# Gate and up products of the feed-forward by one level of Strassen's identity, with the residual parked in DRAM

## The chip, the cores and the metric

The kernel runs on one core of a Trainium2 chip. The metric is the device time of one execution in microseconds (us), as the median of several executions. Five engines work side by side on the core: TensorE (PE in the profile, its weight loads PEld), VectorE (DVE), ScalarE (ACT), GpSimd (POOL) and SyncE (SP), which here only issues DMAs. They meet through semaphores alone.

## The reference

Two layers of a decoder trunk over 512 tokens of 1024 channels, in float32. Each layer has two feed-forward halves around a mixer of four attention branches:

```python
def swiglu(h, w_i, w_o):
    gate, up = jnp.split(h @ w_i, 2, axis=-1)     # h 512 x 1024, w_i 1024 x 5632
    return (jax.nn.silu(gate) * up) @ w_o         # w_o 2816 x 1024

for l in range(DEPTH):                            # DEPTH = 2
    x = x + 0.5 * swiglu(rms_norm(x, ffn1_norm[l]), ffn1_w_in[l], ffn1_w_out[l])
    ...                                           # one projection, four attentions, gates
    x = x + merged @ w_out[l]
    x = x + 0.5 * swiglu(rms_norm(x, ffn2_norm[l]), ffn2_w_in[l], ffn2_w_out[l])
```

The change concerns `h @ w_i`, which is computed four times (two per layer).

## The kernel before

**Layout.** Channels lie on the 128 partitions and tokens along the free axis, so the residual `x` is eight tiles of 128x512 (`NK` = 8), and they stay in SBUF. All products are made at float32 accuracy out of three passes of the `fp32r` type: each operand is split into a high part and a low remainder, and `mm3` (L231 to L236) adds high x high (L234), high x low (L235) and low x high (L236) into one PSUM tile. A weight tile of 128x512 holds four 128x128 blocks; `load_split` (L141) loads it by SP's queue (`raw`, 3 buffers), makes the high part on ACT (L147) and the low part on DVE (L150: raw minus high, both in SBUF). While `lo_parts["shared"]` is set, which is in the mixers only, every second low part is made on POOL.

**Feed-forward** (`ffn`, L253). The 2816 hidden channels are 22 blocks of 128 (`NH`). For each block `j`, called a unit here, `pg` gets 8 x 3 matmuls of 512 columns for the gate and `pu` as many for up. DVE multiplies both by `rb`, the reciprocal of the root mean square of each token (L265, L267), ACT takes the silu (L266), DVE multiplies gate and up (L268), and the result is split into `fh` (ACT, L271) and `fl` (DVE, L272). After the 22 units come eight output tiles `po` of 22 x 3 matmuls each, added to the residual (L278). The output phase already builds the operands of the stage after it: `Norm.add` squares each new residual tile into `ssq` (L181, L182) and splits it, scaled by the gain of the norm, into `xh` and `xl` (L188, L189). `Norm.finish` turns `ssq` into `rb` by one matmul with ones (L196), a square root on ACT (L198) and a reciprocal on DVE (L199).

**Order.** A scheduler places the instructions of each engine; the weight splits have a higher priority (`HP`), so that they run ahead as far as the four buffers of high and low parts allow. Each engine then takes its instructions strictly in that order.

The profile's names end in a letter for the half of a layer: `pga`, `pua`, `poa` belong to the first feed-forward of a layer, `pgb`, `pub`, `pob` to the second.

## Time and profile before

| | us |
|---|---|
| median of 3 executions (2688.86 to 2689.61) | 2688.99 |
| the profiled execution's own time | 2689.76 |
| its span, first to last instruction | 2688.0 |
| TensorE busy | 2669.4 |
| VectorE busy | 1486.0 |
| ScalarE busy | 1326.1 |
| GpSimd busy | 318.9 |

The four feed-forwards lie at about 8 to 375, 989 to 1349, 1349 to 1709 and 2324 to 2688 us of the span; between them are the two mixers with their output products. Busy time is the union of the instructions' own times. A matmul's own time is longer than its distance from the next one, because matmuls are pipelined; what a matmul costs in a full queue is the distance between two starts. `[… <-ACT xhf L188]` at the end of a row gives the idle time ahead of an instruction and what ended it.

### The profile page before, as it was taken

To read this page: it belongs to the slowest core of one execution; us is meant where nothing else is said; L and a number is where in the kernel's file an instruction comes from. 1 tells how busy PE (TensorE), PEld (TensorE's weight loads), DVE (VectorE), ACT (ScalarE), POOL (GpSimd) and SP (SyncE) were. 2 spreads that over 40 slices of the span, in tenths; PEclk is the share of its full clock that TensorE was granted. 3 is DMA by queue.
4 is the path that set the end of the run, shared out by engine and by line. 5 is a ranking of instruction groups with operands and counts; after the bars stand their busy time and mean duration, and the time that the engine had idled before them with its cause. 6 is when DMAs were issued, how large, how long until landed. Compare 5 with 4: busy or idle time off the path is not lost.

```text
span 2688.0 us, 36812 instructions
## 1 busy us (share of the span) xinstructions
PE 2669.4 (99%) x13054; PEld 2266.4 (84%) x13054; DVE 1486.0 (55%) x3028; ACT 1326.1 (49%) x2740; POOL 318.9 (12%) x438
## 2 busy tenths in 40 slices
PE   9999999999999999999999999999999999999999
PEld 7888889888888788888888888998888887888887
DVE  6444437777764564444354443487776646644432
ACT  4333347777665653333333333477776556433321
POOL 1000012222222200000000000222222222000000
PEclk9999999999999999999999999999999999999999
DMA  5333432222322332233322233322223223322233
GB/s 169 99 98 93 118 117 73 75 72 88 88 76 81 101 114 97 96 98 95 98 98 96 97 101 112 113 69 78 76 84 92 69 87 106 110 98 98 96 109 90
DMA packets 146488, 257.10 MB, mean 96 GB/s; under 512 B 17081, under 2 KB 47801, under 8 KB 146304
## 3 DMA queue, kind: packets, MB, share of 16 engines
q1 hardware_dynamic: 138960, 233.16, 28.1%
q0 software_dynamic: 6192, 19.50, 2.5%
q8 instruction: 102, 1.67, 0.3%
q10 hardware_dynamic: 1152, 2.10, 0.2%
q14 instruction: 82, 0.67, 0.1%
HBM read 248.31 MB, written 8.61 MB: 96 GB/s over the span
## 4 chain that ended last, share of the span: by engine, by line
PE 97%; DVE 1%; ACT 1%; issue 1%; DMA 0%; POOL 0%; ACTq 0%; POOLq 0%
PE pgl L234 4%; PE pgl L236 4%; PE pgl L235 4%; PE pga L235 3%; PE pua L234 3%; PE pua L236 3%; PE pua L235 3%; PE pga L236 3%; PE pga L234 3%; PE pob L236 3%; PE pub L234 3%; PE pgb L234 3%; PE pub L236 3%; PE poa L236 3%; PE pgb L236 3%; PE poa L235 3%
## 5 line engine op out<-in xcount | busy, mean ns | idle before, releaser
L234 PE MATMUL pgl<-xhm,higl 128*128 128x512 f32 x512 | 216.4, 423 | 0.0
L236 PE MATMUL pgl<-xhm,logl 128*128 128x512 f32 x512 | 200.9, 392 | 0.0
L235 PE MATMUL pgl<-xlm,higl 128*128 128x512 f32 x512 | 200.2, 391 | 0.0
L234 PE MATMUL pga<-xhf,higa 128*128 128x512 f32 x352 | 138.1, 392 | 3.0 <-ACT xhf L188 3.0
L150 DVE TENSOR_TENSOR loob<-rawob,hiob 128x512 fp32r<-128x512 f32 x96 | 62.0, 646 | 140.6 <-ACT hiob L147 140.6
L234 PE MATMUL pua<-xhf,hiua 128*128 128x512 f32 x352 | 137.9, 392 | 0.0
L235 PE MATMUL pga<-xlf,higa 128*128 128x512 f32 x352 | 137.4, 391 | 0.4 <-DVE xlf L189 0.4
L147 ACT ACTIVATE hiob<-rawob 128x512 fp32r<-128x512 f32 x96 | 57.3, 597 | 163.2 <-PE pob L235 138.3
L234 PE MATMUL pgb<-xhf,higb 128*128 128x512 f32 x352 | 137.8, 391 | 0.0
L235 PE MATMUL pua<-xlf,hiua 128*128 128x512 f32 x352 | 137.5, 391 | 0.0
L236 PE MATMUL pga<-xhf,loga 128*128 128x512 f32 x352 | 137.4, 390 | 0.0
L236 PE MATMUL pua<-xhf,loua 128*128 128x512 f32 x352 | 137.4, 390 | 0.0
L235 PE MATMUL pub<-xlf,hiub 128*128 128x512 f32 x352 | 137.0, 389 | 0.0
L234 PE MATMUL pub<-xhf,hiub 128*128 128x512 f32 x352 | 137.0, 389 | 0.0
L235 PE MATMUL pgb<-xlf,higb 128*128 128x512 f32 x352 | 137.0, 389 | 0.0
L236 PE MATMUL pub<-xhf,loub 128*128 128x512 f32 x352 | 137.0, 389 | 0.0
L235 PE MATMUL pob<-flb,hiob 128*128 128x512 f32 x352 | 136.9, 389 | 0.0
L234 PE MATMUL pob<-fhb,hiob 128*128 128x512 f32 x352 | 136.9, 389 | 0.0
L234 PE MATMUL poa<-fha,hioa 128*128 128x512 f32 x352 | 136.9, 389 | 0.0
L236 PE MATMUL poa<-fha,looa 128*128 128x512 f32 x352 | 136.9, 389 | 0.0
L236 PE MATMUL pgb<-xhf,logb 128*128 128x512 f32 x352 | 136.9, 389 | 0.0
L235 PE MATMUL poa<-fla,hioa 128*128 128x512 f32 x352 | 136.9, 389 | 0.0
(663 smaller groups left out, 7371.1 us busy)
## 6 DMA issues: line engine op xcount, KB each, us to landing
rawgl<-in_w_gate SPq DMA_DIRECT2D x128, 256.0 KB, 2.7
rawga<-in_f_in SPq DMA_DIRECT2D x88, 256.0 KB, 2.7
rawua<-in_f_in SPq DMA_DIRECT2D x88, 256.0 KB, 2.8
rawgb<-in_f_in SPq DMA_DIRECT2D x88, 256.0 KB, 2.7
rawub<-in_f_in SPq DMA_DIRECT2D x88, 256.0 KB, 2.8
rawoa<-in_f_out SPq DMA_DIRECT2D x80, 256.0 KB, 2.6
rawob<-in_f_out SPq DMA_DIRECT2D x80, 256.0 KB, 2.6
rawmo<-in_w_out SPq DMA_DIRECT2D x32, 256.0 KB, 2.8
```

The source lines that it names most:

```text
L147: A.activation(hi[:, :n], raw[:, :n], AF.Copy)
L150: eng.tensor_tensor(lo[:, :n], raw[:, :n], hi[:, :n].bitcast(F32), ALU.subtract)
L234: T.matmul(ps, wh, xh, start=first, stop=False)
L235: T.matmul(ps, wh, xl, start=False, stop=False)
L236: T.matmul(ps, wl, xh, start=False, stop=last)
```

## The change

Gate and up blocks of a unit are put one above the other, and so are the halves of the 1024 channels: the unit's weight is a 2 x 2 array of tiles of 128x512, `a11` and `a12` (gate, first and second half of the channels) and `a21`, `a22` (up). The operand is a 2 x 2 array as well: two halves of the channels (block `m` is paired with block `m + 4`) by two halves of the tokens (256 each). The eight block products are replaced by seven (`a`, `s`, `t`, `b`, `u`, `v`, `d`), each 4 x 3 matmuls of 256 columns:

- the sums of weights s1 to s4 are made on POOL, four additions of 128x512 per unit (L333); all seven weight tiles, four loaded and three or four summed, are then split as before on ACT (L311) and DVE (L312);
- the sums of the operand are made once per norm in `combine` (L224 to L236), which replaces the split for the two feed-forward norms: per pair of blocks, two scaled copies on ACT, four additions of 256 columns on DVE, and four high and low parts (three of 512 columns, one of 256);
- the seven results are added up in `after`: two are copied out of PSUM by ACT (L368, L374), five are read from PSUM by DVE in instructions of 256 columns (L371, L378, L381, L385, L389), two additions of 256 columns go to POOL (L382, L383). The products with `rb`, the silu and the split of the result are as before.

To make room for the seven-part operand, the residual leaves SBUF: it is written to DRAM after each stage and read back tile by tile in the next output phase, by POOL's queue. The merge of the mixer becomes a function of its own with its own buffers.

```diff
-        def split(self, m, xt):
-            g = pv[:, self.l, self.col + m:self.col + m + 1]
...
+            A.activation(r[0], x1, AF.Copy, scale=self.gain(p))
+            A.activation(r[1], x2, AF.Copy, scale=self.gain(p + HK))
+            V.tensor_tensor(r[2][:, lo], r[0][:, lo], r[0][:, hi], ALU.subtract)
+            V.tensor_tensor(r[2][:, hi], r[1][:, hi], r[2][:, lo], ALU.add)
+            V.tensor_tensor(r[3][:, lo], r[1][:, lo], r[2][:, hi], ALU.subtract)
+            V.tensor_tensor(r[0][:, hi], r[0][:, hi], r[1][:, hi], ALU.subtract)
...
+            for n in (0, 2, 1, 3):
+                w = S if n < 3 else TH
+                h = xh[:, n * S:n * S + w]
+                A.activation(h, r[n][:, :w], AF.Copy)
+                V.tensor_tensor(xl[:, n * S:n * S + w], r[n][:, :w], h.bitcast(F32), ALU.subtract)
...
+                    def plus(n, x, y):
+                        t = fp.tile([P, CW], F32, tag="ws", name=f"s{n}{nm}", bufs=4)
+                        with tc.high_priority(offset=HP):
+                            nc.gpsimd.tensor_tensor(t, x, y, ALU.add)
+                        return t
...
+                    s1 = plus(1, a21, a22)
+                    s2 = plus(2, s1, a11)
+                    s3 = plus(3, a11, a21)
+                    s4 = plus(4, s2, a12)
+                    self.w = dict(a=a11, s=s2, t=s1, b=a12, u=s3, v=s4, d=a22)
...
+                        make = (mm_tile, s_tile, mm_tile, t_tile)[made[0] % 4]
+                        self.ps[n] = make(f"p{n}{self.nm}")[:, :TH]
...
+                    for p in pairs:
+                        c = slice(p * P, (p + 1) * P)
+                        T.matmul(ps, wh[:, c], nrm.xh[p][:, sl], start=p == 0, stop=False)
+                        T.matmul(ps, wh[:, c], nrm.xl[p][:, sl], start=False, stop=False)
+                        T.matmul(ps, wl[:, c], nrm.xh[p][:, sl], start=False, stop=p == HK - 1)
...
+                    elif n == "u":
+                        self.dn = half("dn", nm)
+                        V.tensor_tensor(self.dn, ps, self.up, ALU.subtract)
+                        nc.gpsimd.tensor_tensor(self.up, self.up, self.p5, ALU.add)
+                        nc.gpsimd.tensor_tensor(self.u[:, TH:], self.dn, self.p5, ALU.subtract)
+                    elif n == "v":
+                        V.tensor_tensor(self.g[:, TH:], ps, self.up, ALU.add)
...
-                pg = mm_tile(f"pg{name}{j}")
-                chain(pg, w_in[l, j, 0], nrm.xh, nrm.xl, f"g{name}{j}")
-                pu = mm_tile(f"pu{name}{j}")
-                chain(pu, w_in[l, j, 1], nrm.xh, nrm.xl, f"u{name}{j}")
...
-                V.scalar_tensor_tensor(x[m], po, 0.5, x[m], ALU.mult, ALU.add)
...
+                nc.gpsimd.dma_start(xr, x_of[m])
...
+                V.scalar_tensor_tensor(xn, po, 0.5, xr, ALU.mult, ALU.add)
+                (nc.sync if nxt is None and m == NK - 1 else nc.gpsimd).dma_start(keep[m], xn)
```

VectorE within a unit, before, in the second feed-forward of a layer (`lo` are low parts of weights, `ub` and `gb` the results of up and gate, `flb` the low part of the product):

```order
L267 TENSOR_TENSOR ub_11765<-pub_11727,rbf_0_10339 128x512
L150 TENSOR_TENSOR loub_4_11833<-rawub_4_11830,hiub_4_11832 128x512
L268 TENSOR_TENSOR ub_11765<-ub_11765,gb_11764 128x512
L272 TENSOR_TENSOR flb_11771<-ub_11765,fhb_11770 128x512
L150 TENSOR_TENSOR logb_0_11862<-rawgb_0_11859,higb_0_11861 128x512
L265 TENSOR_TENSOR gb_11848<-pgb_11774,rbf_0_10339 128x512
L150 TENSOR_TENSOR logb_4_11880<-rawgb_4_11877,higb_4_11879 128x512
L150 TENSOR_TENSOR loub_0_11899<-rawub_0_11896,hiub_0_11898 128x512
```

Those eight are a whole unit. After the change, in the first feed-forward of a layer, a unit has sixteen; twelve of them in a row (`loaa` is the low part for product `a`, `pua` the result of product `u`, and so on; what ends in `_2849` or less belongs to the unit before):

```order
L312 TENSOR_TENSOR loaa_2950<-waa_2933,hiaa_2949 128x512
L381 TENSOR_TENSOR dna_2885<-pua_2872,upa_2827 128x256
L312 TENSOR_TENSOR losa_2969<-s2a_2943,hisa_2968 128x512
L385 TENSOR_TENSOR ga_2848<-pva_2893,upa_2827 128x256
L386 TENSOR_TENSOR ga_2848<-ga_2848,rbf_0_233 128x512
L312 TENSOR_TENSOR lota_2988<-s1a_2941,hita_2987 128x512
L389 TENSOR_TENSOR ua_2849<-pda_2913,dna_2885 128x256
L312 TENSOR_TENSOR loba_3009<-wba_2939,hiba_3008 128x512
L390 TENSOR_TENSOR ua_2849<-ua_2849,rbf_0_233 128x512
L312 TENSOR_TENSOR loua_3027<-s3a_2945,hiua_3026 128x512
L391 TENSOR_TENSOR ua_2849<-ua_2849,ga_2848 128x512
L371 TENSOR_TENSOR upa_2985<-p1a_2966,psa_2972 128x256
```

The instructions of 256 columns read one operand from PSUM and stand singly between those of 512 columns, which read both from SBUF.

GpSimd around the first feed-forward, before: between the DMAs of the set-up and those that follow the output phase there is nothing.

```order
L332 DMA scr_414<-flat 128x256
L332 DMA scr_416<-flat 128x256
L332 DMA scr_418<-flat 128x256
L332 DMA scr_420<-flat 128x256
L1124 DMA xs_3001<-x_104 128x512
```

GpSimd after, one unit and the start of the next:

```order
L333 TENSOR_TENSOR s1a_2941<-wca_2935,wda_2937 128x512
L333 TENSOR_TENSOR s2a_2943<-s1a_2941,waa_2933 128x512
L333 TENSOR_TENSOR s3a_2945<-waa_2933,wca_2935 128x512
L333 TENSOR_TENSOR s4a_2947<-s2a_2943,wba_2939 128x512
L382 TENSOR_TENSOR upa_2827<-upa_2827,p5a_2846 128x256
L383 TENSOR_TENSOR ua_2849<-dna_2885,p5a_2846 128x256
L333 TENSOR_TENSOR s1a_3099<-wca_3093,wda_3095 128x512
```

All six read both operands from SBUF; L385 on VectorE waits for L382, and L390 for L383.

VectorE where the second feed-forward of layer 0 ends and the first of layer 1 begins, before:

```order
L278 SCALAR_TENSOR_TENSOR xn_10326<-pob_12969,xn_10326 128x512
L150 TENSOR_TENSOR loua_4_13149<-rawua_4_13146,hiua_4_13148 128x512
L182 TENSOR_TENSOR ssqf_1_10342<-ssqf_1_10342,sqf_1_7_13073 128x512
L189 SCALAR_TENSOR_TENSOR xlf_1_7_13077<-xn_10326,pv,xhf_1_7_13076 128x512
L150 TENSOR_TENSOR loga_0_13178<-rawga_0_13175,higa_0_13177 128x512
L199 RECIPROCAL rbf_1_13083<-rbf_1_13083 128x512
```

and after:

```order
L418 SCALAR_TENSOR_TENSOR xnb_16557<-pob_16454,xrb_16452 128x512
L201 TENSOR_TENSOR ssqf_1_15616<-ssqf_1_15616,sqf_1_7_16560 128x512
L226 TENSOR_TENSOR rf_1_3_2_16565<-rf_1_3_0_16563 128x256
L227 TENSOR_TENSOR rf_1_3_2_16565<-rf_1_3_1_16564,rf_1_3_2_16565 128x256
L229 TENSOR_TENSOR rf_1_3_0_16563<-rf_1_3_0_16563,rf_1_3_1_16564 128x256
L228 TENSOR_TENSOR rf_1_3_3_16566<-rf_1_3_1_16564,rf_1_3_2_16565 128x256
L236 TENSOR_TENSOR xlf_1_3_16574<-rf_1_3_1_16564,xhf_1_3_16573 128x512
L236 TENSOR_TENSOR xlf_1_3_16574<-rf_1_3_2_16565,xhf_1_3_16573 128x512
L246 RECIPROCAL rbf_1_16586<-rbf_1_16586 128x512
L236 TENSOR_TENSOR xlf_1_3_16574<-rf_1_3_0_16563,xhf_1_3_16573 128x512
L236 TENSOR_TENSOR xlf_1_3_16574<-rf_1_3_3_16566,xhf_1_3_16573 128x256
L312 TENSOR_TENSOR loaa_16617<-waa_16600,hiaa_16616 128x512
```

The reciprocal, which before stood behind the low parts of the first unit, now stands ahead of the first of them (`loaa`). On TensorE the matmul with ones that feeds it stands directly behind the last matmul of the output phase and ahead of product `a`.

## Rows read from the trace of the kernel before

**Rows 1.** The page: span, engines' busy time, and the chain that ended last.

```profile
span 2688.0 us, 36812 instructions
...
PE 2669.4 (99%) x13054; PEld 2266.4 (84%) x13054; DVE 1486.0 (55%) x3028; ACT 1326.1 (49%) x2740; POOL 318.9 (12%) x438
...
PE 97%; DVE 1%; ACT 1%; issue 1%; DMA 0%; POOL 0%; ACTq 0%; POOLq 0%
```

**Rows 2.** Busy time by stretch: stretch, us, engines (instructions), granted clock, DMA share, GB/s.

```profile
1000.00:1220.00 220.00, 220.00 (x973) 182.21 (x971) 107.50 (x166) 77.89 (x123) 0.00 (x0) 1.00 0.30 99
...
8.40:14.00 5.60, 5.17 (x11) 3.76 (x12) 5.60 (x12) 5.49 (x10) 0.00 (x0) 0.50 0.95 333
```

**Rows 3.** Timeline of TensorE, up product, 512 columns: start us, us, instruction.

```profile
99.69 0.39 PE L235 MATMUL pua<-xlf,hiua 128*128 128x512 f32 x1
...
100.83 0.39 PE L234 MATMUL pua<-xhf,hiua 128*128 128x512 f32 x1
```

**Rows 4.** Timeline of TensorE in a mixer, matmuls of 256 columns.

```profile
779.28 0.28 PE L364 MATMUL pt0d<-hit0d,xlm 128*128 128x256 f32 x1
...
780.12 0.28 PE L362 MATMUL pt0d<-hit0d,xhm 128*128 128x256 f32 x1
```

**Rows 5.** Timeline of VectorE, one unit of a feed-forward.

```profile
1099.38 0.69 DVE L267 TENSOR_TENSOR ub<-pub,rbf 128x512 f32<-128x512 f32 x1 [1.54 <-PE pub L236]
1099.99 0.68 DVE L150 TENSOR_TENSOR loub<-rawub,hiub 128x512 fp32r<-128x512 f32 x1
...
1110.27 0.69 DVE L267 TENSOR_TENSOR ub<-pub,rbf 128x512 f32<-128x512 f32 x1 [1.54 <-PE pub L236]
```

**Rows 6.** Groups of ScalarE in 1000 to 1220 us: count, busy us, mean ns.

```profile
L147 ACT ACTIVATE hiub<-rawub 128x512 fp32r<-128x512 f32 x41 | 25.9, 632 | 67.4 <-PE pub L235 65.0 <-PE pub L236 2.4
```

**Rows 7.** GpSimd: group of 512 columns in the whole span, then one of 256.

```profile
L150 POOL TENSOR_TENSOR logl<-rawgl,higl 128x512 fp32r<-128x512 f32 x64 | 83.6, 1306 | 253.8 <-ACT higl L147 227.9 <-DVE acc L632 13.1 <-DMA rawgl<-in_w_gate 4.7
...
777.46 0.74 POOL L150 TENSOR_TENSOR lot0d<-rawt0d,hit0d 128x256 fp32r<-128x256 f32 x1 [0.87 <-ACT hit0d L147]
```

**Rows 8.** Timelines of VectorE and GpSimd where the two meet in a mixer.

```profile
718.62 1.29 DVE L634 TENSOR_TENSOR acc<-acc,gt 128x512 f32<-128x512 f32 x1
...
718.35 1.02 POOL L150 TENSOR_TENSOR lot0d<-rawt0d,hit0d 128x384 fp32r<-128x384 f32 x1 [4.73 <-ACT hit0d L147]
...
552.87 0.68 DVE L150 TENSOR_TENSOR logl<-rawgl,higl 128x512 fp32r<-128x512 f32 x1
...
553.40 1.30 POOL L150 TENSOR_TENSOR logl<-rawgl,higl 128x512 fp32r<-128x512 f32 x1 [4.67 <-ACT higl L147]
```

**Rows 9.** Single lines of VectorE: duration ns min/median/max, first and last start.

```profile
L632 DVE TENSOR_TENSOR gt<-pbr,gt x48: 670/690/693, 672.4 to 2284.5; 128x512 f32<-128x512 f32 x48
...
L634 DVE TENSOR_TENSOR acc<-acc,gt x48: 671/691/1499, 673.8 to 2285.2; 128x512 f32<-128x512 f32 x48
...
L576 DVE TENSOR_TENSOR o0B<-po0B,oc0B x12: 407/422/428, 541.0 to 661.4; 64x256 f32<-64x256 f32 x12
```

**Rows 10.** Timelines of TensorE and ScalarE at the start.

```profile
8.42 0.80 PE L234 MATMUL pga<-xhf,higa 128*128 128x512 f32 x1 [3.04 <-ACT xhf L188]
...
7.65 0.72 ACT L188 ACTIVATE xhf<-x,pv 128x512 fp32r<-128x512 f32 x1 [2.53 <-DMA pv<-in_pv]
```

**Rows 11.** Timelines between two feed-forwards: TensorE, VectorE, ScalarE.

```profile
1349.42 0.39 PE L234 MATMUL pga<-xhf,higa 128*128 128x512 f32 x1
...
1349.62 0.69 DVE L278 SCALAR_TENSOR_TENSOR xn<-pob,xn 128x512 f32<-128x512 f32 x1 [0.23 <-PE pob L236]
...
1351.01 0.70 DVE L182 TENSOR_TENSOR ssqf<-ssqf,sqf 128x512 f32<-128x512 f32 x1
...
1357.06 0.69 ACT L198 ACTIVATE rbf<-pnf,epsc 128x512 f32<-128x512 f32 x1 [2.96 <-PE pnf L196]
...
1357.78 3.35 DVE L199 RECIPROCAL rbf<-rbf 128x512 f32<-128x512 f32 x1 [4.26 <-ACT rbf L198]
```

More of the change, by code (lines that the diff above doesn't have):

```diff
@@ L168, in __init__, with open, close, order @@
             self.l, self.col, self.name = l, PV[which], name
+            self.pairs = which != "nm"
             self.xh, self.xl = [], []
-            self.ssq = per.tile([P, S], F32, tag="ssq", name=f"ssq{name}")
+            self.kept = {}
+        def open(self):
+            self.pool = tc.tile_pool(name=f"x{self.name}", bufs=1, side="right", reuse_waits="tile")
+            self.xp = self.pool.__enter__()
+            self.ssq = per.tile([P, S], F32, tag="ssq", name=f"ssq{self.name}")
+        def close(self):
+            self.pool.__exit__(None, None, None)
+        def order(self):
+            return [m // 2 + m % 2 * HK for m in range(NK)] if self.pairs else range(NK)
         def add(self, m, xt, alloc):
             self.square(m, xt, alloc)
-            self.split(m, xt)
+            self.split(m, xt, alloc)
         def square(self, m, xt, alloc):
@@ new lines, in ffn @@
+            for j in range(NH):
+                t = Hidden(j)
+                if j == 0:
+                    for n in "ast":
+                        t.product(n, range(HK - 1))
+                for n in "astbuvd":
+                    t.product(n, range(HK - 1, HK) if j == 0 and n in "ast" else range(HK))
+                    t.after(n)
+            nrm.close()
+            if nxt is not None:
+                nxt.open()
+            for n, m in enumerate(nxt.order() if nxt is not None else range(NK)):
+                if n == 1 and early is not None:
+                    early()
+                xr = fp.tile([P, S], F32, tag="g", name=f"xr{name}{m}")
+                nc.gpsimd.dma_start(xr, x_of[m])
@@ L1090, in mixer @@
                 ml.append(lo)
-            xn = []
-            for m in range(NK):
-                xr = sb_tile(f"xr{l}{m}")
+            for m in nxt.order():
+                xr = mp.tile([P, S], F32, tag="xr", name=f"xr{l}{m}", bufs=3)
                 nc.gpsimd.dma_start(xr, xs[m])
@@ L1121, in trunk_kernel @@
         nxt.finish_cols()
[L1122 to L1124 removed]
         nrm, nxt = nxt, Norm(l, "n2", f"f2_{l}")
[L1126 removed]
+        x = kept(f"xt{l}")
+        with tc.tile_pool(name=f"acc{l}", bufs=1, reuse_waits="tile") as ap:
+            acc = []
+            mixer(l, nrm, ap, acc)
+            nrm.close()
+            nxt.open()
+            merge(l, acc, nxt, xs, x)
```

167 lines of the change are left out of this document (115 added, 52 removed).

## The prediction

> **What bounds the kernel now.** The page comes first: TensorE is busy for 2669.4 of 2688.0 us and 97% of the chain that ended last is TensorE; VectorE is busy 55%, ScalarE 49%, GpSimd 12% [rows 1]. A change that takes columns from TensorE therefore pays, as long as nothing else becomes later. The second view is the busy time by stretch, because those shares are averages: in 220 us inside a gate-and-up phase VectorE has 107.50 us, ScalarE 77.89 and GpSimd nothing at all, at a granted clock of 1.00 [rows 2]. GpSimd works in the mixers only. The third view are the timelines of one unit. VectorE's L267 returns after 1110.27 − 1099.38 = 10.89 us [rows 5]; that is one unit, and there are 4 x 22 = 88 of them, 958 us in all. Five matmul starts lie 1.14 us apart, 0.228 us each [rows 3], and 48 of these are 10.94 us: a unit is TensorE's time.
>
> **The change, TensorE.** A unit gets 7 x 4 x 3 = 84 matmuls of 256 columns for 48 of 512. The mixers have such matmuls, each with a weight load of its own as here: seven starts in 0.84 us, 0.120 us each [rows 4]. So 84 x 0.120 = 10.08 us: 0.81 us less per unit, 71 us over 88 (2.6%), and not an eighth of 958, since half the columns cost more than half the time.
> The page "TensorE: Matmul & The Clock Gate" of the Trainium skill (section "Back-to-back issue gap") gives a gap of columns over 2.4 GHz plus 2.5 ns, which is 109 and 216 ns here; by it 84 would be 9.17 us and 48 would be 10.36, an estimate of 104 us saved. The rows show 120 and 228 ns, and they decide.
>
> **VectorE and ScalarE, per unit.** VectorE has eight instructions of 512 columns now. After: seven low parts of weights, and as before `rb` twice, gate times up, and `flb`: eleven of 512 columns, all reading both operands from SBUF, plus five of 256 columns that read one from PSUM. Two that wait for nothing start 1099.99 − 1099.38 = 0.61 us apart [rows 5]; 11 x 0.61 = 6.7 us. The 256-column kind takes 0.42 [rows 9], 0.34 with the same overlap of 0.08; 5 x 0.34 = 1.7. Together 8.4 us, below 10.08. ScalarE: nine of 512 columns at 0.63 [rows 6] and two copies of 256 columns, which cost no more than that each, so at most 11 x 0.63 = 6.9 us. Both would hide under TensorE if each engine stood alone.
>
> **GpSimd, per unit.** Four additions of 512 columns at 1.30 and two of 256 at 0.74 [rows 7, 8]: 6.7 us, which also is below 10.08. But GpSimd and VectorE don't stand alone, and this is the step on which the forecast rests. Where they meet in a mixer, L634 (both operands in SBUF) takes 1.29 instead of its median of 0.69: GpSimd's instruction ends at 718.35 + 1.02 = 719.37, VectorE's at 718.62 + 1.29 = 719.91, 0.54 us later [rows 8, 9]. The other way round, GpSimd starts at 553.40 while VectorE runs until 553.55 and ends at 554.70, 1.15 us after it [rows 8]. So the two exclude each other for 0.54 of VectorE's 0.69 us and for 1.15 of GpSimd's 1.30; only the first 0.15 us of either can lie beside the other. L632, with one operand in PSUM, shows nothing of it: 48 instructions, the longest 0.693, where L634's longest is 1.499 [rows 9]. I take 0.74 − 0.15 = 0.59 for GpSimd's 256 columns.
>
> **The sum for a unit.** Exclusive time: 11 x 0.54 + 4 x 1.15 + 2 x 0.59 = 5.94 + 4.60 + 1.18 = 11.72 us. That alone is above TensorE's 10.08 and above the 10.89 of before. It is the lower bound; it needs all five PSUM instructions and every wait to lie under GpSimd's work. The upper bound lets nothing lie beside anything: 8.41 + 5.78 = 14.19. In between decides VectorE's order. The PSUM instructions stand singly between the others, so a 1.15 us hold can hide one of them (0.34) and then stops the next low part. I let two of the four sums meet one: 4.60 − 0.68 = 3.92. The two small additions stand on a loop: L382 can only start when `dn` (L381) is made, VectorE's L385 waits for it one instruction later, and L383 follows at once and stops L386; I count 0.74 of wait and hold there and 0.15 for the rest, 0.9. So 8.41 + 3.92 + 0.9 = 13.2 us. VectorE then is late for TensorE's low parts, and the four buffers of high and low parts (4 x 12 x 0.120 = 5.8 us of matmuls) run empty within a few units. Per unit 13.2 − 10.89 = +2.31, over 88 units **+203 us**.
>
> **Starts and seams.** Before, the first matmul follows the first split at 8.42 [rows 10], at half the clock: 11 of them in 8.40 to 14.00 [rows 2], worth 2.5 us at full clock, so a full-speed start would be 11.5. After, VectorE's list ahead of the first low part of a weight has 39 instructions: 16 sums of 256 columns (5.4), the low parts of four pairs (12 x 0.61 + 4 x 0.34 = 8.7) and seven squares (4.3), 18.4 us from 7.65 on, and half of the first four sums on GpSimd, 2.3 us: first product at 28.4, **+17**. At the three seams into a paired norm the next product now waits for the whole norm, since on VectorE the reciprocal stands ahead of the first low part: residual 0.23 + 0.69, square 0.63, sum 0.70, root 0.69, reciprocal 3.35 [rows 6, 11], two low parts and the first weight's (0.61 + 0.34 + 0.61), and some 0.5 us (an estimate) for the matmul with ones: 7.8 us and hand-overs, where before the next product had begun 0.2 us before that residual [rows 11]. I take 8.2 each, **+25**. The first unit of each phase finds no weights prepared: 2 us each (an estimate from three low parts), **+8**. I let the residual's reads and writes cost nothing: they are issued in output phases, where an output tile takes 66 x 0.228 = 15 us and GpSimd has no arithmetic. Without that cover a read would cost at most a few us per phase. The mixers' code is the same, 0.
>
> **Sum:** 2688 + 203 + 17 + 25 + 8 = 2941 us of span. The profiled execution's own time was 1.8 above its span and 0.8 above the median of the runs, so a median lies some 1 us above the span: **2942 us**, 9% slower. A measurement of this kernel tells 0.2% (5 us) from no change.
>
> **Rivals.**
> *TensorE stays the bound (the other side).* The exclusion might cost VectorE less: below 10.08 − 8.41 = 1.67 us per unit of the 5.78 that GpSimd holds, VectorE keeps up, and from there TensorE decides: 2688 − 71 + 50 + 1 = 2668 us, faster by 0.8%. For it: all three engines' own sums are below 10.08, and no row of a feed-forward shows GpSimd at work. Against it: exclusive time alone needs 11.72, and L634 and the pair at 553 us fit it to a few hundredths. Chance 0.13.
> *The port at its floor.* If the scheduler's order happens to interleave, a unit is 11.7 to 12.5 us: 2688 + 73 + 30 + 1 = 2792 (with cheaper seams) to about 2880. For it: in the rows GpSimd takes its turn at the next boundary of VectorE's instructions, so neither starves. Against it: VectorE takes its instructions in order. Chance 0.10.
> *Whole instructions exclude each other*, the first 0.15 us too, and VectorE meets every one: 8.41 + 4 x 1.30 + 2 x 0.74 = 15.1 us per unit, 2688 + 370 + 50 + 1 = 3109 us. Rows 8 speak against it, the chain of L382 to L386 for something near it. Chance 0.09.
> The page "SBUF — State Buffer" (section "SBUF: two separate sides") states this as a rule: VectorE's instruction with two SBUF inputs and GpSimd's share a port pair as an exclusive lock for the whole instruction. By that rule the exclusive time of a unit would be 11 x 0.69 + 6.68 = 14.3 us; the rows let 0.15 us of each overlap, hence my 11.72.
> *The clock falls.* TensorE would wait for a quarter of each unit. After 3.04 us without work [rows 10] it was granted 0.50, the 1.2 GHz level [rows 2]. At that level 84 matmuls take some 20 us and the kernel about 3550. Against it: a product of 1.4 us stands between any two waits, and no wait of a unit comes near 3 us. Chance 0.02.
>
> **How the numbers follow.** The forecast (12.5 to 14.2 us per unit, 2880 to 3035) has 0.66. The range of 8 in 10 takes it in, with most of the floor's case and the lower edge of the whole-instruction case: 2790 to 3055. Faster by over 0.2% is the first rival, 0.13; slower are the others, 0.86; 0.01 is left for no change.
>
> **What would show it.** In the profile after: units of VectorE about 13 us apart; low parts (L312) and L386, L390 of up to 1.8 us beside GpSimd's L333, while L378 or L389 stay at 0.4; VectorE nearly without idle time, TensorE's gaps ended by DVE at L312; 256-column starts 0.120 apart within a product. I am wrong if VectorE shows idle time ended by TensorE, if L312's median stays at 0.69 with its longest below 1, or if TensorE's share stays near 99%.

## The result

The changed kernel takes 2956.48 us, median of 4 runs, against 2689.08: a ratio of 1.0992, 95% interval 1.0973 to 1.1011. The forecast was 2942, the range 2790 to 3055. The profiled execution took 2953.4 us with a span of 2951.6, that is 263.6 us over the span of before.

The page of the changed kernel: span, busy time, the chain that ended last, and one of the groups (out<-in, shapes, count, busy us, mean ns, idle time before).

```profile
span 2951.6 us, 46110 instructions
...
PE 2710.2 (92%) x16222; PEld 2392.5 (81%) x16222; DVE 2156.0 (73%) x3828; ACT 1524.5 (52%) x3245; POOL 1052.4 (36%) x1022
...
PE 60%; DVE 24%; issue 12%; POOL 3%; ACT 1%; DMA 0%; DVEq 0%; POOLq 0%; ACTq 0%
...
L333 POOL TENSOR_TENSOR s3b<-wab,wcb 128x512 f32<-128x512 f32 x44 | 73.5, 1670 | 72.7 <-DVE loub L312 72.7
```

Against [rows 1], TensorE's share of the chain fell from 97% to 60%, and VectorE and "issue" (time in which the profile shows no wait) hold most of what it lost. GpSimd's instructions of 512 columns, 1.30 us in [rows 7], now take 1.67 us in the mean of this group. The shares are averages again; the stretch inside one gate-and-up phase says it better. Windows of the changed kernel (as in [rows 2]: stretch, us, TensorE, weight loads, VectorE, ScalarE, GpSimd with instructions, granted clock, DMA share, GB/s):

```profile
1100.00:1320.00 220.00, 184.96 (x1401) 171.01 (x1400) 208.72 (x268) 95.39 (x186) 133.79 (x102) 1.00 0.26 81
1017.50:1022.00 4.50, 4.15 (x9) 2.86 (x10) 4.47 (x9) 3.63 (x7) 0.00 (x0) 0.50 0.12 43
1075.20:1085.00 9.80, 5.93 (x24) 5.32 (x25) 6.28 (x8) 2.46 (x5) 1.28 (x1) 0.50 0.16 54
```

In the first line VectorE is at 208.72 of 220 us, where it had 107.50, TensorE at 184.96, and the clock stays at 1.00. The other two lines are the starts of a merge and of a phase, at half the clock; they come up below.

One unit of VectorE, from one low part of product `t` to the next, and GpSimd beside it (start us, us, engine, line, tiles; in brackets the idle time before it and what ended it). A hold is the time by which an instruction takes longer than it does alone:

```profile
1198.91 1.78 DVE L312 TENSOR_TENSOR lotb<-s1b,hitb 128x512 fp32r<-128x512 f32 x1
1200.61 0.41 DVE L389 TENSOR_TENSOR ub<-pdb,dnb 128x256 f32<-128x256 f32 x1
1200.94 1.71 DVE L312 TENSOR_TENSOR lobb<-wbb,hibb 128x512 fp32r<-128x512 f32 x1
1202.58 0.68 DVE L390 TENSOR_TENSOR ub<-ub,rbf 128x512 f32<-128x512 f32 x1
...
1204.39 0.41 DVE L371 TENSOR_TENSOR upb<-p1b,psb 128x256 f32<-128x256 f32 x1
1204.72 1.45 DVE L312 TENSOR_TENSOR lovb<-s4b,hivb 128x512 fp32r<-128x512 f32 x1
...
1206.70 1.78 DVE L312 TENSOR_TENSOR lodb<-wdb,hidb 128x512 fp32r<-128x512 f32 x1
...
1210.97 0.42 DVE L385 TENSOR_TENSOR gb<-pvb,upb 128x256 f32<-128x256 f32 x1 [0.63 <-POOL upb L382]
1211.43 0.75 DVE L386 TENSOR_TENSOR gb<-gb,rbf 128x512 f32<-128x512 f32 x1
1212.10 1.78 DVE L312 TENSOR_TENSOR lotb<-s1b,hitb 128x512 fp32r<-128x512 f32 x1
```

```profile
1198.40 1.74 POOL L333 TENSOR_TENSOR s1b<-wcb,wdb 128x512 f32<-128x512 f32 x1
1200.82 1.29 POOL L333 TENSOR_TENSOR s2b<-s1b,wab 128x512 f32<-128x512 f32 x1 [0.68 <-POOL s1b L333]
1203.94 1.68 POOL L333 TENSOR_TENSOR s3b<-wab,wcb 128x512 f32<-128x512 f32 x1 [1.83 <-DVE loub L312]
1206.31 1.62 POOL L333 TENSOR_TENSOR s4b<-s2b,wbb 128x512 f32<-128x512 f32 x1 [0.68 <-POOL s3b L333]
```

The unit returns after 1212.10 − 1198.91 = 13.19 us. Four low parts are held, by 1.10, 1.03, 0.77 and 1.10 us over their 0.68, together 4.00. Each ends 0.55 us after the addition that held it: `s1b` ends at 1198.40 + 1.74 = 1200.14, `lotb` at 1200.69. L371, which reads one operand from PSUM, lies wholly under `s3b` and takes its 0.41 us. The one wait of the unit is that of L385 for the small addition on GpSimd, 0.63 us.

Who waited for VectorE in 1080 to 1360 us, one phase (waiter, waited for, us in total, times, longest):

```profile
PE ptb L362 <- DVE lotb L312: 15.7, 19, 0.8
```

Where the 263.6 us lie, by the first TensorE start of each stage before and after (a seam is the place between two stages at which TensorE waits for a norm):

| stage | before | after | more | forecast |
|---|---|---|---|---|
| to the first product | 8.42 | 29.73 | 21.3 | |
| four gate-and-up phases | 967.6 | 1158.4 | 190.9 | |
| setup matmuls, moved from the first phase to its output phase | | | 3.3 | |
| these three together | | | 215.5 | 17 + 203 + 8 = 228 |
| three gaps at the seams | 0 | 10.3 + 7.4 + 10.3 | 28.0 | 25 |
| two mixers and the rest of their merges | 1229.3 | 1249.4 | 20.1 | 0 |

### The profile page after: what moved, and what is told of

Read it like the earlier page. It is cut to its first block, busy times and chain, and to the rows that moved or that the text cites. A ratio compares the mean times of both kernels' runs of the same rounds, so it can differ in the third digit from the quotient of the medians.

```text
span 2951.6 us, 46110 instructions
## 1 busy us (share of the span) xinstructions
PE 2710.2 (92%) x16222; PEld 2392.5 (81%) x16222; DVE 2156.0 (73%) x3828; ACT 1524.5 (52%) x3245; POOL 1052.4 (36%) x1022
## 4 chain that ended last, share of the span: by engine, by line
PE 60%; DVE 24%; issue 12%; POOL 3%; ACT 1%; DMA 0%; DVEq 0%; POOLq 0%; ACTq 0%
PE pgl L281 4%; PE pgl L282 4%; PE pgl L283 4%; PE poa L281 3%; PE poa L283 3%; PE pob L283 3%; PE poa L282 3%; PE pob L282 3%; PE pob L281 3%; DVE lotb L312 2%; DVE lota L312 2%; DVE loda L312 2%; DVE lodb L312 2%; POOL upb L382 1%; POOL upa L382 1%
## 5 line engine op out<-in xcount | busy, mean ns | idle before, releaser
L153 POOL TENSOR_TENSOR logl<-rawgl,higl 128x512 fp32r<-128x512 f32 x64 | 83.0, 1297 | 260.4 <-ACT higl L150 225.9
L153 DVE TENSOR_TENSOR looa<-rawoa,hioa 128x512 fp32r<-128x512 f32 x96 | 62.0, 645 | 122.6 <-ACT hioa L150 120.7
L283 PE MATMUL pob<-fhb,loob 128*128 128x512 f32 x352 | 137.1, 390 | 0.0
L150 ACT ACTIVATE hiob<-rawob 128x512 fp32r<-128x512 f32 x96 | 57.0, 596 | 150.6 <-PE pob L282 132.5
L150 ACT ACTIVATE hioa<-rawoa 128x512 fp32r<-128x512 f32 x96 | 57.0, 596 | 146.1 <-PE poa L282 112.5
L283 PEld LDWEIGHTS pgl<-xhm,logl 128*128 128x128 f32 x512 | 96.4, 188 | 23.1
L281 PEld LDWEIGHTS pgl<-xhm,higl 128*128 128x128 f32 x512 | 97.6, 191 | 17.1
L150 ACT ACTIVATE higl<-rawgl 128x512 fp32r<-128x512 f32 x128 | 80.6, 630 | 58.8 <-PE pgl L282 38.8
L282 PEld LDWEIGHTS pgl<-xlm,higl 128*128 128x128 f32 x512 | 97.3, 190 | 14.2
L394 ACT ACTIVATE fha<-ua 128x512 fp32r<-128x512 f32 x44 | 27.8, 633 | 144.9 <-DVE ua L391 144.9
L394 ACT ACTIVATE fhb<-ub 128x512 fp32r<-128x512 f32 x44 | 27.8, 633 | 144.4 <-DVE ub L391 87.0
L333 POOL TENSOR_TENSOR s3b<-wab,wcb 128x512 f32<-128x512 f32 x44 | 73.5, 1670 | 72.7 <-DVE loub L312 72.7
L333 POOL TENSOR_TENSOR s3a<-waa,wca 128x512 f32<-128x512 f32 x44 | 73.1, 1662 | 73.3 <-DVE loua L312 73.3
```

Source lines behind the costliest of these rows:

```text
L150: A.activation(hi[:, :n], raw[:, :n], AF.Copy)
L153: eng.tensor_tensor(lo[:, :n], raw[:, :n], hi[:, :n].bitcast(F32), ALU.subtract)
L281: T.matmul(ps, wh, xh, start=first, stop=False)
L282: T.matmul(ps, wh, xl, start=False, stop=False)
L283: T.matmul(ps, wl, xh, start=False, stop=last)
L333: nc.gpsimd.tensor_tensor(t, x, y, ALU.add)
```

## The experiments

A unit is the time from one instruction of VectorE to the same one of the next unit, or, where TensorE has no gap, a phase divided by 22.

| run | us | ratio to before (95%) | a unit, us |
|---|---|---|---|
| sums on VectorE | 2772.59 | 1.0308 (1.0292 to 1.0323) | 11.12 |
| no sums | 2693.85 | 1.0015 (1.0006 to 1.0025) | 10.08 |
| copies on GpSimd | 2728.61 | 1.0146 (1.0130 to 1.0163) | 10.46 |
| before, with additions | 2699.06 | 1.0033 (1.0020 to 1.0045) | 10.9 |
| parking alone | 2738.13 | 1.0178 (1.0163 to 1.0194) | 11.24 |
| the same, 32 bytes on | 2716.05 | 1.0098 (1.0083 to 1.0113) | 11.03 |
| the same, 96 bytes on | 2704.02 | 1.0053 (1.0038 to 1.0069) | 10.92 |
| no sums, 32 bytes on | 2678.49 | 0.9956 (0.9942 to 0.9971) | 9.90 |
| sums in PSUM, 32 bytes on | 2684.51 | 0.9977 (0.9968 to 0.9986) | 9.89 |
| the same, late norm, 96 bytes on | 2690.28 | 1.0005 (0.9997 to 1.0014) | 10.08 |
| the same, late norm, 32 bytes on | 2677.73 | 0.9952 (0.9939 to 0.9966) | 9.90 |
| the same, TensorE kept busy | 2680.45 | 0.9964 (0.9952 to 0.9977) | 9.9 |

The first four runs ask whether the shared port is the cause, the next three what parking the residual costs by itself, the others whether the products can win.

### The four sums on VectorE

```diff
-                            nc.gpsimd.tensor_tensor(t, x, y, ALU.add)
+                            V.tensor_tensor(t, x, y, ALU.add)
```

> The changed kernel with one word altered: the four sums of 512 columns per unit (L333) are issued on VectorE instead of GpSimd. Theory (shared port): an addition costs VectorE 0.61 us of its own time, where on GpSimd it cost the pair about 1.0 us of holds (in the changed kernel four low parts per unit stretch by 0.77 to 1.10 us, 4.00 together). A unit becomes 13.19 - 4.00 + 4 x 0.61 = 11.63 us, still VectorE's time: 2956 - 88 x 1.56 = 2819 us, 2795 to 2845, although the engine that is late gets 4 instructions more; low parts go back to 0.69 except where the two small additions on GpSimd meet one. Rival (VectorE is late because it has too much work in order, the stretched durations are records of waits for data): 13.19 + 2.44 = 15.6 us per unit, about 3170 us.

Measured: 2772.59 us, 11.12 per unit. The engine that was late got four instructions more per unit, and the kernel became 184 us faster. The rival, that VectorE merely has too much to do, gave 3170. The number was still missed by 46 us, 0.5 per unit, because I had kept the wait of L385 for GpSimd's small addition (0.63 us). It is gone. VectorE, then GpSimd, in that run:

```profile
1158.13 0.68 DVE L312 TENSOR_TENSOR losb<-s2b,hisb 128x512 fp32r<-128x512 f32 x1
1158.73 0.69 DVE L312 TENSOR_TENSOR lotb<-s1b,hitb 128x512 fp32r<-128x512 f32 x1
1159.33 0.42 DVE L389 TENSOR_TENSOR ub<-pdb,dnb 128x256 f32<-128x256 f32 x1
1159.67 0.90 DVE L312 TENSOR_TENSOR lobb<-wbb,hibb 128x512 fp32r<-128x512 f32 x1
```

```profile
1157.18 2.83 POOL L382 TENSOR_TENSOR upb<-upb,p5b 128x256 f32<-128x256 f32 x1 [7.14 <-DVE dnb L381]
```

The scheduler had put six other instructions between L381 and L385, so nobody waits for L382 any more, although it takes 2.83 us instead of 0.74. It is held while VectorE's two-input instructions follow each other, and ends 1160.01 − 1159.42 = 0.59 us after `lotb`, under the instruction that reads PSUM. VectorE pays 0.22 us for it, in `lobb`.

### No sums at all

```diff
-                    s1 = plus(1, a21, a22)
-                    s2 = plus(2, s1, a11)
-                    s3 = plus(3, a11, a21)
-                    s4 = plus(4, s2, a12)
+                    s1, s2, s3, s4 = a22, a21, a11, a12
```

> The changed kernel without the four sums per unit: the products s, t, u, v take a loaded block in place of a sum, so the output isn't the reference's. All else is as in the changed kernel, the two small additions on GpSimd too. Theory (shared port): VectorE needs 8.41 + 0.78 = 9.2 us per unit, TensorE 84 x 0.120 = 10.08 decides: 2956 - 88 x 3.1 = 2683 us, 2670 to 2715, nearly the time of before, with TensorE at 98% or more inside a phase. Rival (VectorE's order, the waits between products and the buffers hold the unit back, not the port): units of 11 us or more, above 2760 us.

Measured: 2693.85, 11 us over the 2683 and inside the bounds. VectorE in that run, the same instruction of two units that follow each other:

```profile
1149.66 0.41 DVE L368 TENSOR_TENSOR upb<-p1b,psb 128x256 f32<-128x256 f32 x1
...
1159.74 0.41 DVE L368 TENSOR_TENSOR upb<-p1b,psb 128x256 f32<-128x256 f32 x1
```

10.08 us: 84 x 0.120, TensorE's own time, to the hundredth. Everything else of the change is in this run (seven products, two small additions on GpSimd, the PSUM steps), so the 3.1 us per unit that the changed kernel has above it belong to the four sums.

### Copies in place of the sums

```diff
-                            nc.gpsimd.tensor_tensor(t, x, y, ALU.add)
+                            nc.gpsimd.tensor_copy(t, x)
```

> The changed kernel with each of the four sums on GpSimd replaced by a copy of one of its operands (one input instead of two; the output isn't the reference's). No row so far shows a GpSimd instruction with one SBUF input beside VectorE's. Theory A (any SBUF access of GpSimd excludes VectorE's two-input instructions): low parts beside the copies stretch by about the copy's duration less 0.15, a unit is 13.19 less 4 times what a copy is shorter than 1.30 us. If a copy takes 0.6 us: 4.00 us of holds become about 1.4, VectorE 10.6 us, 2956 - 88 x 2.6 = 2727 us. Theory B (only two-input instructions of GpSimd exclude): low parts stay at 0.69, 10.28 us per unit, 2694 us as without the sums.

Measured: 2728.61, where theory A gave 2727 and theory B 2694. GpSimd, then VectorE:

```profile
1158.48 1.08 POOL L333 COPY s1b<-wcb 128x512 f32<-128x512 f32 x1
1160.23 0.62 POOL L333 COPY s2b<-s1b 128x512 f32<-128x512 f32 x1 [0.67 <-DVE lotb L312]
```

```profile
1159.01 1.09 DVE L312 TENSOR_TENSOR lotb<-s1b,hitb 128x512 fp32r<-128x512 f32 x1
```

A copy that meets nobody takes 0.62 us. `lotb` is held by 0.41 us, the four low parts together by 1.25 (0.41, 0.35, 0.08, 0.41), and the unit is 10.46. So one SBUF input on GpSimd's side is enough (a copy writes to SBUF as well), and the hold grows with the length of GpSimd's instruction. The page "SBUF — State Buffer" of the Trainium skill (section "SBUF: two separate sides") states an exclusive lock between VectorE's instructions with two SBUF inputs and those of GpSimd that read SBUF. The three runs agree with it; only its whole instruction is a little less here, since 0.13 to 0.15 us at the start of either lie beside the other.

### The kernel before, with additions for nothing

```diff
             eng.tensor_tensor(lo[:, :n], raw[:, :n], hi[:, :n].bitcast(F32), ALU.subtract)
+            if lo_parts["extra"] is not None:
+                e = lo_parts["extra"].tile([P, CW], F32, tag="ex", name=f"ex{name}", bufs=2)
+                nc.gpsimd.tensor_tensor(e, raw, raw, ALU.add)
...
+            lo_parts["extra"] = fp
             for j in range(NH):
```

> The kernel before with four useless additions of 512 columns per unit on GpSimd (raw weights added to themselves into a spare tile) in the gate-and-up phases. Theory (shared port): VectorE's 4.9 us of a unit become at most 4.9 + 4 x 1.1 = 9.3 us, below TensorE's 10.89, so the time stays at 2689 us within 0.3%, while L150 there rises from 0.69 us to between 1.0 and 1.8 and GpSimd's additions from 1.30 to up to 1.74. Rival (no lock, only records): time the same and L150 at 0.69. Second rival (a low part that is late by 1 us delays TensorE even where VectorE has time left): slower by 1% or more.

Measured: 2699.06, 9 us more. Three of the four phases took 240.27 us, as before, to the hundredth; the first one took 254.21 instead of 246.76, and the first mixer 1.7 more. So GpSimd's work costs nothing while VectorE has time left. The 7.5 us of the first phase are another matter. The kernel before, then this run, in 15 to 30 us, and TensorE in this run:

```profile
15.00:30.00 15.00, 15.00 (x67) 12.22 (x66) 10.24 (x22) 8.68 (x15) 1.06 (x2) 1.00 0.42 124
15.00:30.00 15.00, 12.12 (x32) 5.13 (x30) 12.90 (x22) 9.15 (x14) 8.01 (x8) 0.79 0.25 79
```

```profile
20.94 1.13 PE L199 MATMUL pnf<-ssqf,ones 128*128 128x512 f32 x2 [1.51 <-DVE ssqf L185]
23.44 3.37 PE L325 MATMUL pb<-oh,tab 33*10 33x512 f32 x4 [1.37 <-DMA tab<-in_rel_table]
```

In this build the norm's matmul stands behind 36 matmuls of the products, where the kernel before has it behind 78. TensorE waits there for a sum that VectorE made before the first addition (which starts at 21.01), then for a DMA, and after that runs at a granted clock of 0.50 until about 32 us. So these 7.5 us come with another order of TensorE's work; that the port has a part in them is not shown.

Half of the expectation failed: L150 was hardly held. VectorE's L150 for one tile in a phase (min/median/max ns), and one of the additions:

```profile
L150 DVE TENSOR_TENSOR loub<-rawub,hiub x42: 678/691/810, 1010.7 to 1228.8; 128x512 fp32r<-128x512 f32 x42
```

```profile
1101.85 1.04 POOL L153 TENSOR_TENSOR exub<-rawub 128x512 f32<-128x512 f32 x1 [1.46 <-DMA rawub<-in_f_in]
```

The additions start when a weight lands, and VectorE is idle then for about half of the time. This run therefore shows that such work is free beside an idle VectorE, and nothing on how often the two would meet.

### Parking alone

```diff
-            self.pairs = which != "nm"
+            self.pairs = False
...
-                for n in "astbuvd":
-                    t.product(n, range(HK - 1, HK) if j == 0 and n in "ast" else range(HK))
-                    t.after(n)
+                pg = mm_tile(f"pg{name}{j}")
+                chain(pg, w_in[l, j, 0], nrm.xh, nrm.xl, f"g{name}{j}")
...
```

> The changed kernel with the block products off: plain splits in every norm, gate and up by 48 matmuls of 512 columns as before; the residual parked in DRAM and the merge as a function with its own pool stay. Theory: in the changed kernel the merge began 3.0 us after the last branch matmul and ran its first 9 us at a granted clock of 0.50 to 0.85, which came from the merge's tiles in their own pool, not from the products: 2689 + 2 x 7 = 2703 us, 2698 to 2712; the norms' seams cost nothing without the paired splits. Rival (parking costs nothing, as the prediction had it, and the late merge belongs to the paired norm): 2689 us within 3.

Measured: 2738.13, where I expected 2703 and the rival 2689. The merges began late as expected, but each gate-and-up phase was 247.3 us instead of 240.3, with the very matmuls of before, and TensorE busy all through. The starts had moved apart. What differs is where the norm's tiles lie: the changed kernel puts them in a pool of their own on the right side of SBUF. In this build the first starts at byte 196576 of a partition, 32 over a multiple of 64; in the kernel before it starts at 30336, a multiple of 128. Two runs moved it.

```diff
+    pad = ctx.enter_context(tc.tile_pool(name="pad", bufs=1, side="right"))
+    nc.gpsimd.memset(pad.tile([P, 8], F32, name="pad"), 0.0)
```

> The kernel with parking alone, with one spare tile of 32 bytes ahead of the norm tiles on the right side of SBUF, so that they start at a multiple of 64 bytes (196544) and not at 32 over one (196576). In the run without it, gate and up matmuls of 512 columns started 231 to 237 ns apart where the kernel before has 227, and phases took 247.3 us instead of 240.3, while the output matmuls, whose moving tiles start at a multiple of 64, kept 227. Theory (the start address of the moving tile sets the pitch): 227 again, phases 240.3 and mixers 3 us shorter: 2738 - 4 x 7 - 2 x 3 = 2704 us, 2699 to 2710; what stays over 2690 is the merge's late start, 2 x 7. Rival (which side or how far from the weights the tile lies, or the parked residual's DMAs, set it): stays at 2738.

With 32 bytes: 2716.05, two thirds of the way. The phases went from 247.27 to 242.59 us, not to 240.3.

```diff
-    nc.gpsimd.memset(pad.tile([P, 8], F32, name="pad"), 0.0)
+    nc.gpsimd.memset(pad.tile([P, 24], F32, name="pad"), 0.0)
```

> Parking alone once more, with a spare tile of 96 bytes instead of 32, so that the norm tiles start at a multiple of 128 bytes (196480), as in the kernel before (30336). With 32 bytes they started at 196544, 64 over a multiple of 128, and phases went from 247.3 only to 242.6 us, with starts of 225 to 232 ns. Theory (the moving tile's start address within 128 bytes sets the pitch): 227 ns and phases of 240.3 us, mixers 571 to 574: 2716 - 4 x 2.3 - 2 x 2 = 2703 us, 2698 to 2708. Rival (64 bytes was all that the address gives, the rest comes from the side of SBUF): 2716.

With 96 bytes, so that tiles start at a multiple of 128: 2704.02, and the phases (but for the first, which has set-up work) are 240.27 us again. TensorE in the three runs, two starts each with nine matmuls of 512 columns from one to the other:

```profile
1099.77 0.39 PE L281 MATMUL pgb<-xhf,higb 128*128 128x512 f32 x1
...
1101.87 0.39 PE L281 MATMUL pub<-xhf,hiub 128*128 128x512 f32 x1
```

```profile
1099.98 0.39 PE L283 MATMUL pub<-xhf,hiub 128*128 128x512 f32 x1
...
1102.04 0.39 PE L283 MATMUL pgb<-xhf,higb 128*128 128x512 f32 x1
```

```profile
1100.14 0.39 PE L283 MATMUL pub<-xhf,hiub 128*128 128x512 f32 x1
...
1102.18 0.39 PE L283 MATMUL pub<-xhf,hiub 128*128 128x512 f32 x1
```

2.10, 2.06 and 2.04 us for nine: 0.233, 0.229 and 0.227 us each. Nothing but the start address changed. The address also costs the mixers, 577.4 us against 574.4. What is left of parking is 2704.02 − 2689.74 = 14.3 us, and it is the merge. A low part of the merge, `ml`, in the kernel before, where the merge's matmuls begin at 945.96 without a gap; then TensorE in the changed kernel, the last branch matmul and the first of the merge:

```profile
939.97 0.68 DVE L1088 TENSOR_TENSOR ml<-acc,mh 128x512 fp32r<-128x512 f32 x1
```

```profile
1014.11 0.39 PE L283 MATMUL pbr<-oh0D,lobr 128*128 128x512 f32 x1
1017.54 1.22 PE L281 MATMUL pmo<-mh,himo 128*128 128x512 f32 x2 [3.04 <-ACT mh L1223]
```

The merge's tiles lie in a pool that opens when the mixer's closes, so `mh` comes only now, where before it was made during the last branches. TensorE waits for 3.04 us and then runs at a granted clock of 0.50 (second line of the windows above): 3.2 + 3.9 us, twice, in the run with tiles at a multiple of 128. The residual's DMAs cost nothing: from the second on, the output phases are 119.7 us as before.

### No sums, 32 bytes on

The edit is the spare tile of 32 bytes.

> The changed kernel without the sums (a loaded block in place of each sum, so the output isn't the reference's) and with the same spare tile of 32 bytes. Theory (address): matmuls of 256 columns go from about 120 to 116 ns apart, the lowest that the run without the spare tile showed, a unit from 10.28 to 84 x 0.116 = 9.75 us plus what VectorE's wait for GpSimd adds: 2694 - 88 x 0.5 - 6 = 2644 us, 2635 to 2660. Rival (address without effect): 2694; a third outcome, VectorE at 9.2 us plus waits becoming the bound, would stop the gain between, 2660 to 2680, with TensorE's gaps ended by VectorE.

Measured: 2678.49, less than a third of the expected gain: 9.90 us per unit, 118 ns a start and not 116. TensorE had no gap inside a phase, so VectorE was not the third outcome; the address gives 2 ns.

### The sums in PSUM

```diff
+                        self.Y = mm_tile(f"Y{nm}")[:, :TH]
+                        A.activation(self.U[:, :TH], self.X, AF.Copy, scale=-1.0)
...
-                        V.tensor_tensor(self.up, self.p1, ps, ALU.subtract)
+                        V.tensor_tensor(self.Y, self.p5, self.U[:, :TH], ALU.subtract)
...
-                        T.matmul(ps, wh[:, c], nrm.xh[p][:, sl], start=p == 0, stop=False)
+                        T.matmul(ps, wh[:, c], nrm.xh[p][:, sl], start=fresh and p == 0, stop=False, skip_group_check=True)
...
-                V.scalar_tensor_tensor(xn, po, 0.5, xr, ALU.mult, ALU.add)
+                V.tensor_tensor(xn, po, nrm.rb, ALU.mult)
+                V.scalar_tensor_tensor(xn, xn, 0.5, xr, ALU.mult, ALU.add)
```

> A whole kernel (same output): the weights' four sums on VectorE, no work for GpSimd in a unit; the products b, s, u, v, d add onto what PSUM already holds (ScalarE puts minus the first product there, VectorE the sum for v), the factor rb on up goes to the output tiles, the spare tile of 32 bytes as above. VectorE per unit: 7 low parts, 4 sums, up times gate, flb at 0.602 and four of 256 columns at 0.333: 13 x 0.602 + 4 x 0.333 = 9.16 us. Theory (no lock, VectorE below TensorE): 84 x 0.116 = 9.75 us per unit decides: 2773 - 88 x (11.16 - 9.8) = 2653 us, 2640 to 2675, below the kernel before. Rival (the adding chain makes TensorE wait for ScalarE's and VectorE's 256-column steps, since they stand behind 0.6 us instructions in order): units of 10.5 to 11.2 us, 2715 to 2775.

Measured: 2684.51, between the two expectations. The unit is 9.89 us as the theory had it: TensorE adds five products onto what PSUM holds and waits for nobody. Window of that run, inside a phase:

```profile
1040.00:1220.00 180.00, 180.00 (x1530) 180.00 (x1529) 169.50 (x310) 107.98 (x200) 0.00 (x0) 1.00 0.32 104
```

TensorE is busy all 180 us, GpSimd does nothing, and VectorE is busy for 9.3 of 9.9. The profiled execution took 2678.39 us, 25 more than 2653. Most of them, some 20, lie at the starts of the phases: from its first product on the second phase took 222.3 us where 22 x 9.89 is 217.6, for a phase begins with a wait for the first low part behind the reciprocal and with a granted clock of 0.50 (1010 to 1018 us). About 6 lie in the output phases, 121.2 us where they took 119.7.

One phase of this execution was faster than the other three. Windows of the third phase and of the fourth:

```profile
1440.00:1560.00 120.00, 120.00 (x1061) 120.00 (x1060) 116.51 (x215) 75.30 (x139) 0.00 (x0) 1.00 0.34 111
2400.00:2520.00 120.00, 120.00 (x1021) 120.00 (x1020) 113.24 (x207) 71.58 (x134) 0.00 (x0) 1.00 0.33 107
```

TensorE is busy throughout in both, at the same clock, and the norm's tiles lie at the same addresses; yet the matmuls start 113 ns apart in the third and 118 in the others, which is 8 us in a phase. The run with TensorE kept busy, below, had the 113 ns too, in a part of its fourth phase only. No run here shows the cause.

### The late norm, and the address for 256 columns

```diff
                     t.after(n)
+                    if j == 0 and n == "s":
+                        nrm.finish()
...
-        nxt.finish()
```

> The kernel with the sums in PSUM, with the spare tile at 96 bytes and with the end of a paired norm (matmul with ones, root, reciprocal) issued behind the third product of the first unit instead of ahead of all. In the run without this a seam was 7.2 us of gap, then 2.7 us more until the first low part, which stood behind the reciprocal of 3.35 us, and 8 us at half the clock. Theory: the reciprocal no longer stands ahead of the first low part, so each of three seams loses 3.4 us, some 5 with the clock: 2684 - 3 x 4 = 2672, and the multiple of 128 brings matmuls of 256 columns from 117.8 to 113 to 116 ns: 88 x 84 x 3 ns = 22 us at most, VectorE at 9.2 us per unit still below 84 x 0.113 = 9.5: 2655 us, 2645 to 2675. Rival (the seam's gap is the split of the last pair and the first unit's own sums and low parts, so it stays, and the address gives nothing at 256 columns): 2680 to 2687.

Measured: 2690.28, slower than without. The gaps at the seams fell from 7.2 to 5.2 us, but the units went back to 10.08. Starts of 256 columns in this run, at a multiple of 128 bytes, and then in the next, at 64 over one (twelve matmuls from one row to the other):

```profile
1149.85 0.28 PE L368 MATMUL Ub<-xhf,hisb 128*128 128x256 f32 x1
...
1151.29 0.28 PE L368 MATMUL Xb<-xhf,hibb 128*128 128x256 f32 x1
```

```profile
1149.92 0.28 PE L368 MATMUL Tb<-xhf,hitb 128*128 128x256 f32 x1
...
1151.33 0.28 PE L368 MATMUL Ub<-xhf,hisb 128*128 128x256 f32 x1
```

1.44 and 1.41 us for twelve: 120 and 118 ns. What is best for 512 columns is not best for 256.

> The late norm with the spare tile back at 32 bytes: norm tiles 64 over a multiple of 128 bytes, as in the run with the sums in PSUM. At a multiple of 128 all 256-column starts were 120 ns apart (10.08 us per unit), at 64 over it 113 to 119 (9.89). Theory (the two widths want different starts: 512 columns a multiple of 128, 256 columns 64 over it): 9.9 us per unit again, 2690 - 88 x 0.18 = 2674, 2668 to 2679. Rival (the slower unit came from the moved reciprocal, not from the address): 2690.

Measured: 2677.73, 4 us over the 2674. Only the spare tile differs from the run before, and in each of the two runs all four phases keep to one distance, 120 ns there and 118 here: the address was the cause. This is the fastest whole kernel here, 0.9952 of the kernel before (0.9939 to 0.9966), 0.5% faster.

```diff
+    def busy(n, x, name):
+        d = psa.tile([P, S], F32, tag="t", name=f"busy{name}")
+        for _ in range(n):
+            T.matmul(d[:, :P], ones, x[:, :P], start=True, stop=True)
+    busy(112, ones, "0")
...
+                if m == NK - 1:
+                    busy(22, t, f"m{l}")
```

> The same with matmuls of 128 columns whose result nobody reads: 112 of them at the start, and 22 at each of three seams, which wait for the last residual tile of the norm and stand ahead of the first product. At the seams TensorE was idle for 5.2 to 5.9 us and then worked at a granted clock of 0.50 for about 6 us, at the start for 20.6 us and some 8 us after. Theory (a TensorE kept at work keeps its clock): 6 us at half the clock cost 3 us, so 3 at each seam and 4 at the start: 13 us less than without, 2661, 2655 to 2668. Rival (VectorE's list sets the first units anyway, so the clock gives back 1 to 4 us in all): 2670 to 2673. Second rival (the idle matmuls end late and hold the first product): above 2675.

Measured: 2680.45, in the bounds of the second rival. No gain that can be told, though the clock did what was asked of it. Windows of that run at a seam:

```profile
1004.00:1009.50 5.50, 5.50 (x46) 5.02 (x45) 5.28 (x12) 3.45 (x7) 0.00 (x0) 1.00 0.13 49
...
1012.00:1015.00 3.00, 1.61 (x14) 1.41 (x13) 3.00 (x4) 2.99 (x6) 0.00 (x0) 1.00 0.66 215
```

The clock is 1.00 from the first product on, and then TensorE is busy for 1.61 of 3.00 us, with VectorE at 3.00: the first unit is VectorE's list (sums, low parts, reciprocal) at this clock too. From the end of the merge to the first output product it took 228.1 us, as without. The extra matmuls also held the first product, by 0.5 us at each seam and by 4.2 at the start (32.0 against 27.8).

## Why the prediction was right, point by point

**The bound.** It said that VectorE and GpSimd together, not TensorE, would set a unit. In [rows 5] VectorE had waited 1.54 us for TensorE; now the only idle time of its unit is 0.63 us, ended by GpSimd, and in one phase 19 products `t` wait for a low part, 15.7 us in all. The run without sums and the one with the sums on VectorE show that it was the sums, and where they run.

**The unit, 13.2 us.** Measured 13.19, and by its own terms: VectorE's list 11 x 0.602 + 5 x 0.333 = 8.29 (8.41 forecast), holds 4.00 (3.92), and 0.9 (0.9) for the wait of L385 and what the small additions hold. The forecast let two of the four sums run beside an instruction that reads PSUM. That was a choice and not worked out, and it was lucky by a little: only L371 does so wholly, under `s3b` (its low part is held by 0.77), L389 partly under `s2b` (1.03), and a full hold is 1.10 where it took 1.15. The two errors, less hidden and shorter holds, nearly cancel. So the two-sided reading of [rows 8, 9] carried to a stretch in which neither engine had worked beside the other. The low end (11.72) needed all five PSUM instructions and every wait to lie under GpSimd's work, and did not come.

**TensorE, 84 x 0.120.** 10.08 us, exact in the run without sums. It was luck in part: the mixers' 120 ns [rows 4] were read from tiles that start elsewhere; 118 can be had, and 113 was seen in one phase. The page "TensorE: Matmul & The Clock Gate" of the Trainium skill (section "Back-to-back issue gap") gives the formula that the prediction set beside it (109 and 216 ns) for a matmul by itself, not for a stream of them; no term rested on it.

**Start and first units.** The first product came at 29.7 (28.4 forecast). The 8 us for four first units are not there: phases two to four are 290 us, 22 x 13.19. A first unit does lose, since its first low part came at 1078.14, after the first product; but in the last unit no sums run for a next one, and its low parts are 0.68 again. The forecast counted one end of the pipeline and not the other. With the units this is 215.5 against 228.

**Seams.** 28.0 against 25, which is luck in part. The terms that the forecast lists add up to 8.3 us and not 7.8, and the largest of them, the reciprocal of 3.35 us, doesn't lie in the gap. TensorE starts again behind ScalarE's high part of the first weight (`hiab` below) and waits for VectorE's list with the reciprocal only at its third matmul (`loab`, 2.88 us), inside the phase. The gap holds two things instead that the forecast left out: a table load ahead of the root on ScalarE, and, behind the merges, the holds of GpSimd's first sums on the split of the last pair (10.3 us of gap there, 7.2 in the run without sums). TensorE at the seam, then ScalarE:

```profile
1075.20 0.58 PE L360 MATMUL pab<-xhf,hiab 128*128 128x256 f32 x1 [5.04 <-ACT hiab L311]
...
1078.88 0.58 PE L362 MATMUL pab<-xhf,loab 128*128 128x256 f32 x1 [2.88 <-DVE loab L312]
```

```profile
1071.82 1.28 ACT L245 ACT_TABLE_LOAD   x1
```

**Mixers: "the code is the same, 0".** This step failed: 20.1 us. The code that computes is the same, but the tiles are not where they were. Of the 20.1, 6 come from the start address of the norm's tiles (577.4 against 574.4, by the runs with parking alone) and most of the rest from the merge's own pool (3.2 us of gap and up to 3.9 at half the clock, twice). These 20.1 us too few and the 12.5 too many for start, phases and first units cancel in good part; the total of 2942 is nearer to 2956 than its parts deserve.

**Parking, "costs nothing".** True of its DMAs, untrue of what the parking made room for: 14.3 us for the pools, by the run with tiles at a multiple of 128, and 48 with the tiles where the change had put them. That is the price for plain products of 512 columns; in the changed kernel the address costs only the mixers, 6 us. No view of the kernel before showed the address as a price.

## What to carry to other kernels

Add up not only each engine's instructions but also those of two engines that exclude each other: here three engines needed 10.08, 8.4 and 6.7 us each, and the unit took 13.2. An addition that costs GpSimd 1.30 us can cost a busy VectorE 1.0 us of holds, more than the 0.60 that it takes there, so work for GpSimd belongs beside an idle VectorE. After a change of layout, look first whether untouched matmuls still start as far apart as before: matmuls of 512 columns lost 3% of a phase here when their tiles started at another address.
